# Modulation weights of pairs 1 to 7 in 2 MB chunks with buffers of their own, and two chunks at the RWKV block's entry

## The chip, the core and the metric

The kernel runs on one core of one Trainium2 chip. The metric is the device time of one execution in microseconds. The engines that matter: TensorE (PE in the profile: products; PEld: its weight loads), VectorE (DVE), ScalarE (ACT), GpSimd (POOL) and SyncE (SP), whose queue issues most loads.

## The reference, cut to what matters

One inference step of a two-layer trunk for 256 prompt tokens and 8 sequences of 8 sample tokens, together 320 columns (T), with 1024 features (8 tiles of 128). Everything is float32. Each layer is a feed-forward part, a token mixer (layer 0: RG-LRU, layer 1: RWKV-7) and a second feed-forward part. Every sub-layer takes a normed input with shift, scale and gate that come from a conditioning vector c:

```python
mod = (jax.nn.silu(c) @ P['ada_w'][layer] + P['ada_b'][layer]).reshape(B, N_MOD, D_MODEL)
sh1, sc1, g1, sh2, sc2, g2, sh3, sc3, g3 = [mod[:, m, None, :] for m in range(N_MOD)]
x = x + FFN_RES * (1.0 + g1) * swiglu(modulate(x, sh1, sc1), P['ffn_w_in'][layer, 0], P['ffn_w_out'][layer, 0])
h = modulate(x, sh2, sc2)
...   # y = the token mixer of h
x = x + (1.0 + g2) * y
x = x + FFN_RES * (1.0 + g3) * swiglu(modulate(x, sh3, sc3), P['ffn_w_in'][layer, 1], P['ffn_w_out'][layer, 1])
```

There are 9 conditioning rows (1 prompt, 8 samples) and 18 modulation vectors of 1024 for both layers. Their weights are 2 x 1024 x 9216 float32, 75 MB, the largest single weight beside the feed-forward ones.

## The kernel before, in words

The program is a list of items. An item has weight blocks and a function that issues its instructions. `Weights` loads the blocks, in the order of the items, through SyncE's queue into a ring of 5 raw buffers of 512 KB (`rawp`, L64). Blocks of dense products are then split into two exact parts, hi on ScalarE (L75) and lo on VectorE (L76), with two pairs of buffers; modulation blocks are used as they come and hold their raw buffer until their products are done. A load waits until the buffer five blocks back is free.

A dense product (`mm3`, L163 to L165) is three passes over 8 tiles of the contraction, 24 products of 128 x 128 weights with 320 (or 330) columns for a block.

The modulation vectors are made in 9 pairs (p = 0 to 8; p holds vectors 2p and 2p + 1), long before each is used. A pair has 8 steps, one for a tile of the contraction. A step (`Ada.step`) has two blocks, one for each vector of the pair, and four products (L179): the silu of c as weights of 32 columns, 512 columns of the block as the moving side, and each product writes its own 32 of the 128 rows of one PSUM bank. After the last step VectorE copies the sums (`ada_sb`, L184), and `finish` turns them with four products (L191) and adds the bias on VectorE (L197, L203).

Pair 0 is made first. The steps of the others are spread as items between those of the big parts (`interleave`): pairs 1 and 2 in the first half of layer 0's first feed-forward part, pair 3 in the RG-LRU block, pairs 4 and 5 in layer 0's second feed-forward part, pair 6 in layer 1's first one. Pairs 7 and 8 are thread "A" of the RWKV block. There, the string `MID` says which thread takes the next step: R, v, V are projections, p0 to p7 the preparation of the eight feature tiles, I, s, X, D, Z the inverse of triangular blocks (s on VectorE, X on TensorE), a0 to a7 the samples, C and G the chunks of the recurrence.

A scheduler then sets each engine's order from the items' order and its own estimate of when operands are there, so the instructions of neighbouring items can mix; after that every engine works its queue in order.

The entry of the RWKV block: the last out product of layer 1's first feed-forward part (`outm`), the residual, the squares on ScalarE (L244), two products with ones (L247, L248) for the norm's sums, then `start` with loads of constants on ScalarE's queue (L610) and the root and reciprocal (L265, L266), then `hd` and `part` for the first two tiles on VectorE, ScalarE and GpSimd, and `k_outer` (L833 to L837), the first products.

In `prep` (p0 to p7) the tile kk has one buffer: VectorE writes it (L769), ScalarE copies it into Dp (L780), and TensorE reads Dp (g, L803) and kk (dt, L822).

## Time and profile before

| | |
|---|---|
| time, median of 3 runs | 1502.36 us (1501.66 to 1503.32) |
| the profiled execution, first to last instruction | 1503.8 us (the page gives this span and no other time of its own) |
| TensorE busy | 1451.2 us, 97% |
| VectorE, ScalarE busy | 868.5 us (58%), 672.7 us (45%) |
| modulation products (L179) | 576 records, 101.1 us of TensorE |
| loads | 256.31 MB on SyncE's and ScalarE's hardware queue 1, 51.4% of the 16 DMA engines' time |

In rows of groups stands: line, engine, operation, what is written and read, shapes, count, then busy time and the mean of one in ns, then the idle time before them and who ended it. A row of the timeline is start, length, engine, line, names, count, and in brackets the idle time before it. A row of stretches is the stretch, its length, then for PE, PEld, DVE, ACT and POOL the busy time with the number of instructions in brackets, then the granted TensorE clock as a share of full speed, the share of the DMA engines and GB/s; where such a view is for one line, it holds only the engines which that line uses. A float32 product leaves two records in the trace, a product with the split parts one.

### The profile page before, as it was taken

How to read it: one execution, taken by the hardware profiler on the slowest of the kernel's cores; microseconds unless marked ns; L12 is line 12 of the kernel's file. 1: busy time of each engine (PE TensorE's matmuls, PEld its weight loads, DVE VectorE, ACT ScalarE, POOL GpSimd, SP SyncE). 2: the span in 40 equal slices, each digit the busy share in tenths (PEclk: the TensorE clock that was granted, in tenths of full speed). 3: DMA queues.
4: the chain of work that ended last, by engine and by line, in shares of the span. 5: the costliest groups of instructions: out<-in, count | busy, mean ns of one | idle time of the engine just before them, and what ended most of it. 6: DMA issues, size and time to landing. Idle time of an engine off the chain costs nothing.

```text
span 1503.8 us, 26002 instructions
## 1 busy us (share of the span) xinstructions
PE 1451.2 (97%) x10408; PEld 1306.0 (87%) x10408; DVE 868.5 (58%) x1667; ACT 672.7 (45%) x1215; POOL 65.1 (4%) x173
## 2 busy tenths in 40 slices
PE   5999999999999999999999997999998999999997
PEld 1888899988989889999999997597766779999996
DVE  6544445588874345566444447686763589544444
ACT  4433333487553333444333334475435446444432
POOL 0000000021000000000000003000022010000000
PEclk9999999999999999999999998999999999999998
DMA  8666744466467664545564545224765144444452
GB/s 338 234 244 239 247 138 152 151 231 224 153 233 248 238 242 140 154 152 201 205 223 140 151 140 173 102 90 159 219 207 177 51 147 141 142 153 154 139 148 72
DMA packets 93881, 266.58 MB, mean 177 GB/s; under 512 B 26368, under 2 KB 28800, under 8 KB 93248
## 3 DMA queue, kind: packets, MB, share of 16 engines
q1 hardware_dynamic: 84688, 256.31, 51.4%
q10 hardware_dynamic: 8976, 8.35, 1.7%
q8 instruction: 81, 1.33, 0.4%
q0 software_dynamic: 96, 0.26, 0.1%
q14 instruction: 40, 0.33, 0.1%
HBM read 257.86 MB, written 7.03 MB: 176 GB/s over the span
## 4 chain that ended last, share of the span: by engine, by line
PE 87%; DVE 6%; ACT 2%; DMA 2%; issue 1%; POOL 1%; ACTq 0%; DVEq 0%; SPq 0%; POOLq 0%
PE po L165 8%; PE po L163 8%; PE po L164 8%; PE pg L163 7%; PE pu L163 7%; PE pg L165 7%; PE pg L164 7%; PE pu L165 7%; PE pu L164 7%; PE ada_ps L179 5%; PE g L803 1%; DVE lo L76 1%; PE ps_l L687 1%; PE ps_p L163 1%; PE ps_p L165 1%
## 5 line engine op out<-in xcount | busy, mean ns | idle before, releaser
L75 ACT CAST hi<-raw 128x1024 fp32r<-128x1024 f32 (+1 forms) x334 | 341.8, 1023 | 613.2 <-issue 195.1
L76 DVE TENSOR_TENSOR lo<-raw,hi 128x1024 fp32r<-128x1024 f32 (+1 forms) x334 | 398.2, 1192 | 351.8 <-ACT hi L75 350.5
L163 PE MATMUL po<-hh,hi 128*128 128x320 f32 x704 | 217.2, 309 | 0.0
L165 PE MATMUL po<-hh,lo 128*128 128x320 f32 x704 | 217.2, 309 | 0.0
L164 PE MATMUL po<-hl,hi 128*128 128x320 f32 x704 | 217.2, 309 | 0.0
L163 PE MATMUL pu<-mh,hi 128*128 128x320 f32 x608 | 189.3, 311 | 0.7 <-ACT hi L75 0.7
L163 PE MATMUL pg<-mh,hi 128*128 128x320 f32 x608 | 189.8, 312 | 0.0
L165 PE MATMUL pg<-mh,lo 128*128 128x320 f32 x608 | 187.6, 309 | 0.0
L165 PE MATMUL pu<-mh,lo 128*128 128x320 f32 x608 | 187.6, 309 | 0.0
L164 PE MATMUL pg<-ml,hi 128*128 128x320 f32 x608 | 187.6, 308 | 0.0
L164 PE MATMUL pu<-ml,hi 128*128 128x320 f32 x608 | 187.6, 308 | 0.0
L163 PEld LDWEIGHTS po<-hh,hi 128*128 128x128 f32 x704 | 132.0, 187 | 0.0
L165 PEld LDWEIGHTS po<-hh,lo 128*128 128x128 f32 x704 | 132.0, 187 | 0.0
L164 PEld LDWEIGHTS po<-hl,hi 128*128 128x128 f32 x704 | 132.0, 187 | 0.0
L163 PEld LDWEIGHTS pg<-mh,hi 128*128 128x128 f32 x608 | 114.0, 187 | 16.8 <-issue 16.8
L163 PEld LDWEIGHTS pu<-mh,hi 128*128 128x128 f32 x608 | 114.0, 187 | 11.9 <-issue 8.4
L165 PEld LDWEIGHTS pg<-mh,lo 128*128 128x128 f32 x608 | 114.0, 187 | 0.8 <-DVE u L380 0.8
L164 PEld LDWEIGHTS pu<-ml,hi 128*128 128x128 f32 x608 | 114.0, 188 | 0.0
L164 PEld LDWEIGHTS pg<-ml,hi 128*128 128x128 f32 x608 | 114.0, 188 | 0.0
L165 PEld LDWEIGHTS pu<-mh,lo 128*128 128x128 f32 x608 | 114.0, 187 | 0.0
L179 PE MATMUL ada_ps<-raw,sct 128*32 128x512 f32 x576 | 101.1, 613 | 11.6 <-ACT sct L1277 7.2
L356 DVE TENSOR_TENSOR u<-pu,g 128x320 f32<-128x320 f32 x76 | 37.4, 492 | 109.7 <-PE pu L165 109.6
(358 smaller groups left out, 2375.6 us busy)
## 6 DMA issues: line engine op xcount, KB each, us to landing
raw<-in_ffn_in SPq DMA_DIRECT2D x176, 512.0 KB, 3.6
raw<-in_ada_w SPq DMA_DIRECT2D x144, 512.0 KB, 4.2
raw<-in_ffn_out SPq DMA_DIRECT2D x64, 512.0 KB, 3.6
raw<-in_ffn_out SPq DMA_DIRECT2D x32, 384.0 KB, 3.1
raw<-in_rkv SPq DMA_DIRECT2D x18, 512.0 KB, 4.2
raw<-in_lru_in SPq DMA_DIRECT2D x16, 512.0 KB, 4.2
raw<-in_lru_out SPq DMA_DIRECT2D x8, 512.0 KB, 3.3
raw<-in_wkv SPq DMA_DIRECT2D x8, 512.0 KB, 4.6
```

The source lines that it names most:

```text
L75: self.nc.scalar.copy(out=hi[:, :n], in_=raw[:, :n])
L76: self.nc.vector.tensor_tensor(out=lo[:, :n], in0=raw[:, :n], in1=hi.bitcast(F32)[:, :n], op=ALU.subtract)
L163: nc.tensor.matmul(ps[:, :n], a, xh[:, k0 + k, :n], start=st, stop=False)
L164: nc.tensor.matmul(ps[:, :n], a, xl[:, k0 + k, :n], start=False, stop=False)
L165: nc.tensor.matmul(ps[:, :n], b, xh[:, k0 + k, :n], start=False, stop=sp)
L179: nc.tensor.matmul(self.ps[r:r + 32, :], sct[:, k, :], wh[:, q * 512:q * 512 + 512], start=(k == 0), stop=(k == NT - 1))
L356: nc.vector.tensor_tensor(out=u, in0=pu[:, :T], in1=st[key, "g"], op=ALU.mult)
L687: nc.tensor.matmul(o[:, :T], lw[:, c0:c1], t, **kw)
L803: nc.tensor.matmul(g[:, c - c0, h], Dp[:, c, h].rearrange("p e t -> p (e t)"), AR[:, c].rearrange("p e t -> p (e t)"), start=True, stop=True)
```

## The change

Pairs 1 to 7 no longer go through the raw ring. Their weights load as chunks: 4 to a pair, numbered n = 0 to 27, each two steps and both vectors, 2 MB in one load on SyncE's queue, into two buffers taken in turn (tags MPa and MPb of a new pool `ext`). These two tags were buffers of the RWKV block's pool; their later users there (`xm` of r, MP, zh, zl) now take them from `ext`. The load of chunk n is an item of its own, put three items behind the products of chunk n - 2, but at most 12 items ahead of its own products. The 8 products of a chunk are issued with high priority and kept in program order.

Chunks 24 and 25 (the first half of pair 7) go into layer 1's first feed-forward part behind pair 6; chunk 26 is issued by the norm between the last out product and the two products with ones; chunk 27 by the RWKV block's `start`, after the norm. The copy of pair 7's sums then waits for the last tile of k's operands (`copy7`), and its `finish` stands between the adapters' products (lora). In `MID` the ten A entries of pair 7 are gone and nothing else. Pair 8 stays as it was, in single blocks. To make room, the RG-LRU block's yh and yl take the buffers of xch and xcl.

```diff
+    ext = ctx.enter_context(tc.tile_pool(name="ext", bufs=1))
...
-        def step(self, w, k):
+        def step(self, w, k, copy=True):
             for h, wh in zip(self.halves, w):
                 for q in range(2):
                     r = 64 * h + 32 * q
-                    nc.tensor.matmul(self.ps[r:r + 32, :], sct[:, k, :], wh[:, q * 512:q * 512 + 512],
-                                     start=(k == 0), stop=(k == NT - 1))
-            if k == NT - 1:
...
+                    mm = nc.tensor.matmul(self.ps[r:r + 32, :], sct[:, k, :], wh[:, q * 512:q * 512 + 512],
+                                          start=(k == 0), stop=(k == NT - 1))
+                    tc.keep_in_program_order(mm)
+            if k == NT - 1 and copy:
+                self.copy()
...
                 if self.sc is None and i == NT - 1:
+                    if self.hook:
+                        self.hook()
                     self.ps = bank(6, [128, 512], "st_ps")
...
+    def chunk_load(n):
+        p, c = 1 + n // 4, n % 4
+        t = st["chunk", n] = ext.tile([128, 2, 2, 1024], F32, tag=("MPa", "MPb")[n % 2], name="ada_w")
+        nc.sync.dma_start(out=t, in_=I["ada_w"][p, 2 * c:2 * c + 2].rearrange("k h r n -> r k h n"))
+
+    def chunk_step(n, copy=True):
+        p, c = 1 + n // 4, n % 4
+        if c == 0:
+            st["ada", p] = Ada(p, (0, 1), stat)
+        t = st.pop(("chunk", n))
+
+        with tc.high_priority():
+            for k in range(2):
+                st["ada", p].step([t[:, k, h] for h in range(2)], 2 * c + k, copy)
...
+    def with_loads(items):
+
+        at = {chunks[fn]: j for j, (_, fn, *_) in enumerate(items) if fn in chunks}
+        before = {}
+        for n in sorted(at):
+            lo = at[n - 2] + 3 if n > 1 else at[0] - 4 + 2 * n
+            before.setdefault(max(min(lo, at[n]), at[n] - 12), []).append(n)
...
-            for n, dt in (("xc", F32), ("xch", F32R), ("xcl", F32R), ("r", F32), ("a", F32), ("th", F32), ("gb", F32), ("yh", F32R), ("yl", F32R)):
-                L[n] = P.tile([128, NT, T], dt, name="L" + n)
+            for n, dt in (("xc", F32), ("xch", F32R), ("xcl", F32R), ("r", F32), ("a", F32), ("th", F32), ("gb", F32)):
+                L[n] = P.tile([128, NT, T], dt, tag=n, name="L" + n)
...
+            if i == 0:
+                for n, tag in (("yh", "xch"), ("yl", "xcl")):
+                    L[n] = L["p"].tile([128, NT, T], F32R, tag=tag, name="L" + n)
...
             st["norm"].finish()
+            chunk_step(27, copy=False)
...
+        def copy7(w):
+            with tc.issue_after(R["lo", NT - 1]):
+                st["ada", 7].copy()
+
+        it(copy7)
         for i in range(NT):
+            if i == 2:
+                it(lambda w: st["ada", 7].finish())
             it(lambda w, i=i: lora(w, i))
...
-        for p in (7, 8):
-            if p == 8:
-                step("A", lambda w: st.update(ada_bank=3))
-            for bl, fn in ada_items(p):
-                step("A", fn, bl)
+        step("A", lambda w: st.update(ada_bank=3))
+        for bl, fn in ada_items(8):
+            step("A", fn, bl)
...
-    items.extend(interleave(a, ada_items(1) + ada_items(2), 2, 40))
+    items.extend(interleave(a, ada_chunks(1) + ada_chunks(2), 2, 42))
...
-    items.extend(interleave(lru, ada_items(3), 1, 33))
+    items.extend(interleave(lru, ada_chunks(3), 1, 33))
...
-    items.extend(interleave(a, ada_items(4) + ada_items(5), 2, 40))
+    items.extend(interleave(a, ada_chunks(4) + ada_chunks(5), 2, 42))
...
-    a, b = ffn_items(1, 0, 11, lambda: Norm())
-    items.extend(interleave(a, ada_items(6), 2, 40))
+    a, b = ffn_items(1, 0, 11, lambda: Norm(hook=lambda: chunk_step(26)))
+    items.extend(interleave(a, ada_chunks(6) + [chunk_item(n) for n in (24, 25)], 2, 42))
...
+    items = with_loads(items)
```

How this moves instructions is shown at three places. In the rows stand line, operation, what is written and read, shape, a count, and whose semaphores it waits for. The line numbers of the changed kernel differ: L179 becomes L180, L163 to L165 become L164 to L166, L803 becomes L857, L822 L876, L247 and L248 L254 and L255.

TensorE in layer 0's first feed-forward part, at the first stop for pair 1 (pu and pg are dense products). Before, and then now:

```order
L165 MATMUL pu<-xh,lo 128x330
L179 MATMUL ada_ps<-raw,sct 32x512 [waits DMAHW7_49,PE_49]
L179 MATMUL ada_ps<-raw,sct 32x512
L179 MATMUL ada_ps<-raw,sct 32x512 [waits DMAHW0_49]
L179 MATMUL ada_ps<-raw,sct 32x512
L163 MATMUL pg<-xh,hi 128x330 [waits Activation_49]
```

```order
L165 MATMUL pu<-xl,hi 128x330
L166 MATMUL pu<-xh,lo 128x330
L180 MATMUL ada_ps<-ada_w,sct 32x512 [waits DMAHW4_49,PE_49]
L180 MATMUL ada_ps<-ada_w,sct 32x512 x7
L164 MATMUL pg<-xh,hi 128x330 [waits Activation_49]
```

A stop had one step, four products with a wait for each of two loads; now it has two steps, eight products behind one wait, and there are half as many stops.

TensorE at the RWKV block's entry (po: the last out product; st_ps: the norm's sums; ps_k: k). Before, and then now:

```order
L165 MATMUL po<-hh,lo 128x320
L247 MATMUL st_ps<-acc,ones 128x320
L248 MATMUL st_ps<-sq,ones 128x320 [waits Activation_49]
L833 MATMUL ps_k<-xmxh,hi 128x320 [waits PE_49,Activation_49]
L834 MATMUL ps_k<-xmxh,lo 128x320 [waits DVE_49]
```

```order
L166 MATMUL po<-hh,lo 128x320
L180 MATMUL ada_ps<-ada_w,sct 32x512 [waits DMAHW7_49]
L180 MATMUL ada_ps<-ada_w,sct 32x512 x7
L254 MATMUL st_ps<-acc,ones 128x320
L255 MATMUL st_ps<-sq,ones 128x320 [waits Activation_49]
L180 MATMUL ada_ps<-ada_w,sct 32x512 [waits DMAHW5_49]
...
L887 MATMUL ps_k<-xmxh,hi 128x320 [waits PE_49,Activation_49]
```

Chunk 26 stands ahead of the statistics and chunk 27 (whose other seven products are left out) behind them. On ScalarE's queue the load of c_mask moves ahead of the last squares, and that of c_reset, which was issued earlier in the program, now stands between c_shift and the root.

TensorE in the RWKV block's preparation, between the g products of one tile and of the next (zw, za, pb, pn, dt, g: products of `prep`; ps_p: a projection, here of v). Before, and then now:

```order
L822 MATMUL dt<-eye,kk 128x128 x4
L179 MATMUL ada_ps<-raw,sct 32x512 [waits DMAHW1_49]
L822 MATMUL dt<-eye,kk 128x128 [waits Activation_49]
...
L179 MATMUL ada_ps<-raw,sct 32x512 [waits DMAHW2_49]
...
L741 MATMUL zw<-zwa,raw 128x320 [waits DMAHW5_49,DVE_49]
L179 MATMUL ada_ps<-raw,sct 32x512 [waits DMAHW6_49]
L793 MATMUL pb<-pr,c_bones 128x320 [waits DVE_49]
...
L743 MATMUL za<-zwa,raw 128x320 [waits Activation_49]
```

```order
L876 MATMUL dt<-eye,kk 128x128 x4
L795 MATMUL zw<-zwa,raw 128x320 [waits DMAHW3_49,DVE_49]
L164 MATMUL ps_p<-xmxh,hi 128x320
L876 MATMUL dt<-eye,kk 128x128 [waits Activation_49]
L165 MATMUL ps_p<-xmxl,hi 128x320
L166 MATMUL ps_p<-xmxh,lo 128x320
...
L847 MATMUL pb<-pr,c_bones 128x320 [waits DVE_49]
...
L797 MATMUL za<-zwa,raw 128x320 [waits Activation_49]
```

Where products of pair 7 stood between those of `prep`, products of the v projection stand now, which came further behind before.

More of the change, by code (lines that the diff above doesn't have):

```diff
@@ L178, in step, with copy @@
                     r = 64 * h + 32 * q
-                    nc.tensor.matmul(self.ps[r:r + 32, :], sct[:, k, :], wh[:, q * 512:q * 512 + 512],
-                                     start=(k == 0), stop=(k == NT - 1))
-            if k == NT - 1:
-                self.sb = self.pool.tile([128, 512], F32, tag="ada_sb", name="ada_sb")
-                r0, r1 = 64 * self.halves[0], 64 * self.halves[-1] + 64
-                nc.vector.tensor_copy(self.sb[r0:r1], self.ps[r0:r1])
+                    mm = nc.tensor.matmul(self.ps[r:r + 32, :], sct[:, k, :], wh[:, q * 512:q * 512 + 512],
[3 more added lines that the diff above has]
+                self.copy()
+        def copy(self):
+            self.sb = self.pool.tile([128, 512], F32, tag="ada_sb", name="ada_sb")
+            r0, r1 = 64 * self.halves[0], 64 * self.halves[-1] + 64
+            nc.vector.tensor_copy(self.sb[r0:r1], self.ps[r0:r1])
         def finish(self):
@@ L287, in fn @@
                     st["ada", p] = Ada(p, halves, stat)
-                st["ada", p].step(w, k)
+                with tc.high_priority():
+                    st["ada", p].step(w, k)
             out.append(([(I["ada_w"][p, k, h], False, 1024) for h in halves], fn))
@@ L292, in ada_items, with chunk_item, ada_chunks @@
         out.append(([], lambda w: st["ada", p].finish()))
+        return out
+    chunks = {}
+    def chunk_load(n):
[7 more added lines that the diff above has]
+        t = st.pop(("chunk", n))
+        with tc.high_priority():
+            for k in range(2):
+                st["ada", p].step([t[:, k, h] for h in range(2)], 2 * c + k, copy)
+    def chunk_item(n, fn=None):
+        fn = fn or (lambda w: chunk_step(n))
+        chunks[fn] = n
+        return [], fn
+    def ada_chunks(p):
+        return [chunk_item(4 * (p - 1) + c) for c in range(4)] + [([], None), ([], lambda w: st["ada", p].finish())]
+    def with_loads(items):
[4 more added lines that the diff above has]
+            before.setdefault(max(min(lo, at[n]), at[n] - 12), []).append(n)
+        out = []
+        for j, it in enumerate(items):
+            out.extend(([], lambda w, n=n: chunk_load(n)) for n in before.get(j, ()))
+            out.append(it)
         return out
@@ L412, in ffn_items @@
                           lambda w, m=m, k0=k0, nk=nk: outm(w, m, k0, nk)))
+        if l == 1 and s == 0:
+            chunks[b[-1][1]] = 26
         return a, b
@@ L628, in start @@
             st["norm"].finish()
-        it(start)
+            chunk_step(27, copy=False)
+        out.append(chunk_item(27, start))
         def hd(w, i):
@@ L704, in part_r @@
             if i == 0:
-                R["xm", 0] = pair((big, "x"), (R["p"], "MPb"))
+                R["xm", 0] = pair((big, "x"), (ext, "MPb"))
             part(i, 0, R["xm", 0])
@@ L719, in prep_start @@
             R["bv"] = P.tile([128, NT, T], F32, tag="bv", name="bv")
-            R["MP"] = {0: P.tile([128, 32, 2, 64], F32, tag="MPa", name="MP")}
+            R["MP"] = {0: ext.tile([128, 32, 2, 64], F32, tag="MPa", name="MP")}
             R["Dt"] = {}
@@ L734, in prep @@
             if i == 4:
-                R["MP"][1] = R["p"].tile([128, 32, 2, 64], F32, tag="MPb", name="MP")
+                R["MP"][1] = ext.tile([128, 32, 2, 64], F32, tag="MPb", name="MP")
             MP, MS = R["MP"][i // 4][:, 8 * (i % 4):8 * (i % 4) + 8], R["MS"][:, 2 * i:2 * i + 2]
@@ L1196, in comb @@
                 nc.scalar.dma_start(out=O["wkv_p"], in_=R["Su"])
-                R["zh"] = R["p"].tile([128, NT, T], F32R, tag="MPa", name="zh")
-                R["zl"] = R["p"].tile([128, NT, T], F32R, tag="MPb", name="zl")
+                R["zh"] = ext.tile([128, NT, T], F32R, tag="MPa", name="zh")
+                R["zl"] = ext.tile([128, NT, T], F32R, tag="MPb", name="zl")
                 R["pgs"] = bank(3, [128, NT, 64], "pgs")
```

17 lines of the change are left out of this document (8 added, 9 removed).

## The prediction

> **What bounds the kernel now.** I read the busy table of the page first, then its costliest groups.
>
> ```profile
> span 1503.8 us, 26002 instructions
> PE 1451.2 (97%) x10408; PEld 1306.0 (87%) x10408; DVE 868.5 (58%) x1667; ACT 672.7 (45%) x1215; POOL 65.1 (4%) x173
> L179 PE MATMUL ada_ps<-raw,sct 128*32 128x512 f32 x576 | 101.1, 613 | 11.6 <-ACT sct L1277 7.2
> ```
>
> TensorE (PE) is occupied for 97% of the span, so nearly everything that leaves its queue shortens the run. The third line is what the change touches: the modulation products at L179, 576 records (a float32 product leaves two records: 288 products), 101.1 us. Next, the entry of the RWKV block in the timelines of TensorE and ScalarE (ACT; ACTq is its queue issuing a load):
>
> ```profile
> 910.96 0.70 PE L247 MATMUL st_ps<-acc,ones 128*128 128x320 f32 x2
> 912.46 0.81 PE L248 MATMUL st_ps<-sq,ones 128*128 128x320 f32 x2 [0.80 <-ACT sq L244]
> 920.26 0.63 PE L833 MATMUL ps_k<-xmxh,hi 128*128 128x320 f32 x1 [6.99 <-ACT xmxh L663]
> ...
> 911.94 0.47 ACT L244 ACTIVATE sq<-x 128x320 f32<-128x320 f32 x1
> 913.42 0.45 ACTq L610 DMA_DIRECT2D c_shift<-in_shift  x1
> 913.92 0.53 ACT L265 ACTIVATE rstd<-st_ps,eps 128x320 f32<-128x320 f32 x1 [1.51 <-PE st_ps L248]
> ```
>
> There is one hole of 6.99 us, between the norm's statistics and the first k product, the longest of the span behind the start. ScalarE's root (rstd) starts at 913.92 although the statistics ended at 913.27: ScalarE's queue was still issuing loads until 913.87.
>
> **What one stop for modulation costs.** The timeline of TensorE around a stop in the first feed-forward part, then a stop of one product, and one of two steps together:
>
> ```profile
> 177.42 0.30 PE L165 MATMUL pu<-mh,lo 128*128 128x320 f32 x1
> 177.65 1.07 PE L179 MATMUL ada_ps<-raw,sct 128*32 128x512 f32 x8
> 178.65 0.41 PE L163 MATMUL pg<-mh,hi 128*128 128x320 f32 x1
> 178.90 0.31 PE L164 MATMUL pg<-ml,hi 128*128 128x320 f32 x1
> 179.05 0.31 PE L165 MATMUL pg<-mh,lo 128*128 128x320 f32 x1
> ...
> 300.19 1.05 PE L179 MATMUL ada_ps<-raw,sct 128*32 128x512 f32 x2
> ...
> 1033.71 1.92 PE L179 MATMUL ada_ps<-raw,sct 128*32 128x512 f32 x16
> 1035.56 0.49 PE L822 MATMUL dt<-eye,kk 128*128 128x128 f32 x2
> ```
>
> Dense products follow each other every 0.15 us (178.90 to 179.05). From the last one before the stop (177.42) to the second after it (178.90) are 1.48 us, where two steps of 0.154 would be 0.31: **a stop costs 1.17 us**. A stop of one product (x2) is occupied as long as one of four (1.05 against 1.07): the four products of a step write four groups of 32 rows and run side by side. Two steps together take 1.85 us to the next product, where one takes 1.00 (177.65 to 178.65): the second costs 0.85, so **a chunk costs 2.02 us** against 2.34 for two stops. How many stops each stage has comes from the busy time of L179 alone:
>
> ```profile
> 36.00:190.00 154.00, 17.05 (x128) 2.52 (x128) 0.98 0.69 239
> ...
> 300.00:362.00 62.00, 10.43 (x64) 1.75 (x64) 1.00 0.66 233
> ...
> 410.00:560.00 150.00, 18.09 (x128) 2.65 (x128) 1.00 0.69 240
> ...
> 670.00:790.00 120.00, 9.56 (x64) 1.39 (x64) 1.00 0.59 205
> ...
> 950.00:1066.00 116.00, 12.26 (x64) 1.98 (x64) 1.00 0.39 130
> 1066.00:1135.00 69.00, 15.59 (x64) 2.27 (x64) 1.00 0.70 211
> ```
>
> The first number after the stretch's length is TensorE's busy time. Divided by 1.06 it gives 16 stops, then 8 and one of two steps (8.48 + 1.92 = 10.4), 17, 9, ten (8 of one step or less, 2 of two), and 14.
>
> **The sum, stage by stage.** *Layer 0's first feed-forward part* (pairs 1, 2): 16 stops at 1.17 = 18.7 become 8 chunks at 2.02 = 16.2: **-2.5**. *Layer 0's second part* (pairs 4, 5): 17 stops = 19.9 become 16.2: **-3.7**. *Layer 1's first part*: 9 stops = 10.5 become four chunks of pair 6 and two of pair 7 = 12.1: **+1.6**. These stages have TensorE full, so I take the terms at face value, within 0.5 us in all:
>
> ```profile
> 36.00:190.00 154.00, 153.80 (x1026) 137.03 (x1026) 74.31 (x117) 57.96 (x93) 0.00 (x0) 0.98 0.69 239
> ...
> 400.00:700.00 300.00, 300.00 (x2016) 278.81 (x2015) 171.10 (x309) 128.53 (x212) 2.60 (x6) 1.00 0.60 199
> ```
>
>
> *RG-LRU block* (pair 3): nine stops, 8 x 1.17 + 2.02 = 11.4, become four, 8.1: -3.3. After its double stop TensorE also waits, and then its clock drops:
>
> ```profile
> 359.96 0.42 PE L163 MATMUL pb<-xh,hi 128*128 128x330 f32 x1 [1.53 <-ACT hi L75]
> ...
> 359.30:362.60 3.30, 1.76 (x9) 1.25 (x10) 3.30 (x8) 2.81 (x6) 0.21 (x2) 1.00 0.99 382
> 362.70:366.00 3.30, 3.30 (x14) 3.30 (x13) 3.18 (x9) 0.92 (x2) 2.03 (x2) 0.50 1.01 361
> 366.10:369.40 3.30, 3.30 (x23) 3.30 (x23) 1.96 (x4) 1.67 (x4) 0.00 (x0) 1.00 0.54 164
> ...
> 300.00:400.00 100.00, 97.00 (x616) 85.85 (x615) 85.59 (x216) 75.07 (x152) 18.32 (x44) 0.98 0.59 207
> ```
>
> The 1.53 us come from a late split of a weight block, whose buffer the modulation blocks had held; these no longer share the buffers. In the half-clock stretch (0.50) 14 products ran instead of 23, so 9 x 0.15 = 1.3 us. If both go, the gain is 3.3 + 1.5 + 1.3 = 6.1. Against that, VectorE (the third busy time of a row) works 85.6 of 100 us there, so it may become the limit. Bounds 2 and 6.1; I take **-4.0**, the middle.
>
> *RWKV entry.* Chunk 26 (2.0 us) goes between the last out product and the statistics. It starts where the first statistics product stood (910.96), so that product follows near 913.0 and the second, which waited for ScalarE's squares until 912.46, near 913.3: the statistics end 0.8 later, at about 914.1. ScalarE's queue carries one load issue more (c_reset, 0.45 as c_shift) and would start the root at about 914.35 in any case. Chunk 27 then lies in the hole of 6.99 us, whose end VectorE and ScalarE set. Price: **+0.4** (0 to 1). If the hole gave no cover, chunk 27 would add 2.0.
>
> *RWKV body.* Pair 7 leaves: ten stops, 8 x 1.17 + 2 x 2.02 = 13.4. Pair 8 comes in 12 stops instead of 14: 1.8. If TensorE stayed full, the gain would be 15.2. But its work there hangs on chains of VectorE. The prep of a tile writes kk (L769) into a single buffer, which the dt products of the tile before must have read, and then the inverse runs on VectorE:
>
> ```profile
> 1003.46 0.49 DVE L769 SCALAR_TENSOR_TENSOR kk<-tk,AR 128x320 f32<-128x320 f32 x1 [2.57 <-PE dt L822]
> ...
> 1011.81 0.48 DVE L769 SCALAR_TENSOR_TENSOR kk<-tk,AR 128x320 f32<-128x320 f32 x1
> ...
> 1024.47 0.49 DVE L769 SCALAR_TENSOR_TENSOR kk<-tk,AR 128x320 f32<-128x320 f32 x1 [1.39 <-PE dt L822]
> ...
> 1036.09 0.49 DVE L769 SCALAR_TENSOR_TENSOR kk<-tk,AR 128x320 f32<-128x320 f32 x1 [1.79 <-PE dt L822]
> ...
> 1044.68 0.48 DVE L769 SCALAR_TENSOR_TENSOR kk<-tk,AR 128x320 f32<-128x320 f32 x1
> ...
> 1114.85 0.19 DVE L891 TENSOR_TENSOR X<-X,tm 128x31 f32<-128x31 f32 x1
> ...
> 1118.42 0.74 PE L950 MATMUL xt<-eye,X 64*32 64x64 f32 x10
> ```
>
> Rounds of kk without a stop take 8.35 and 8.59 us, those with stops 12.66 and 11.62 (the latter holds four, 5.5 us): the stops lie on the path, but a round will not fall far under 8.4. The changed order also pulls products of v (24 x 0.154 = 3.7 us each) into those rounds, where the stops were. That work is then missing behind, where TensorE reaches the first product of X 3.4 us after VectorE has finished X (1115.04 to 1118.42). So at least 3 us should be gained, and at most 15.2. I take **-8.5**, a little under the middle, because the copy of pair 7's sums and its six small additions now also fall into the adapters' products (about 1.6 us of VectorE).
>
> Sum: -2.5 - 3.7 + 1.6 - 4.0 + 0.4 - 8.5 = **-16.7**. The profiled span is 1503.8, 1.4 above the median of the runs shown, 1502.4. So 1487.1 for a profiled span and **1485.7 us for the median**; I write 1485.5. Bounds for the median: with -2, +1 and -3 in the unsure terms 1494; with -6.1, 0 and -15.2 1476.5.
>
> **Loads.** The 2 MB loads go into SyncE's queue between the weight blocks, and each waits there until the products of the chunk two before have read its buffer.
>
> ```profile
> raw<-in_ffn_in SPq DMA_DIRECT2D x176, 512.0 KB, 3.6
> ...
> SPq L64 <- DVE lo L76: 828.6, 306, 8.6
> ...
> 915.70:919.00 3.30, 0.00 (x0) 0.00 (x0) 3.11 (x9) 1.09 (x2) 0.96 (x3) 0.50 0.95 374
> ```
>
> A weight load leaves when a split (lo, L76) frees its buffer. With five buffers and two split pairs it is about four blocks, 4 x 3.7 = 14.8 us, ahead of its own split, and lands in 3.6, so 11.2 us may lie ahead of it. 2.1 MB at the 374 GB/s of the last row are 5.6 us. I cost the loads at nothing; the number of bytes is the same as before.
>
> **Rivals.** *A: VectorE takes over.* The RG-LRU and RWKV blocks keep their length and only the feed-forward parts and the entry move: -2.5 - 3.7 + 1.6 + 0.4 = -4.2, 1498. For it: 85.6 of 100 us busy in the RG-LRU, the 8.4 us rounds. Against: rounds with stops are longer by just about the stops' cost. Chance 0.11.
>
> *B: slower, through SyncE's queue.* If a 2 MB load moves no faster than four single ones (4 x 3.6 = 14.4 us), every weight load behind it comes 3.2 us late, 26 times in the dense stretches: 83 us, so about 1570. It decides from 187 GB/s downwards (2.1 MB in 11.2 us). Against: 374 GB/s above. Chance 0.03. The Trainium skill bears on it ("DMA: Bandwidth & Descriptors", Queues, rings and completion order): each DMA engine consumes the descriptors of one issuing engine's ring in order. So a weight block cannot overtake the chunk ahead of it; by this only the lead in time protects it.
>
> *C: the clock holds at the entry.* If chunk 27 kept TensorE's clock up, some 22 k products would run at 0.15 instead of 0.27 us, 2.6 less: 1483. The traces speak against it: 359.30:362.60 shows TensorE busy 1.76 of 3.3 us, and half clock behind it. After chunk 27 some 4.5 us stay empty, so some stretch of 3.3 us has under 1.7 busy. Chance 0.04. The Trainium skill ("TensorE: Matmul & The Clock Gate", What's actually happening) says that half rate comes after at least one idle window of about 3.4 us. Taken as a window with no work at all, it would let the clock hold in part of the cases. The row at 359.30 disagrees, with a drop behind a window half at work, and the measurement decides.
>
> **How the numbers follow.** Forecast 0.82 (a gain of 8 to 26 us), A 0.11, C 0.04, B 0.03. The range is 1477 to 1495, the forecast's bounds; A and B are outside, C inside. 0.2% (3 us) is about what a measurement can tell from no change. Faster holds the forecast, C and most of A: 0.94; same 0.03, for the part of A that also loses the feed-forward gain; slower 0.03, B.
>
> **What would show it.** Right: 24 stops of 16 records before the RWKV block, each 1.9 us busy; 16 records in the hole after the statistics, and the first k product 0 to 1 us later behind the last out product; feed-forward parts shorter by 2.5 and 3.7 us; no half clock inside the RG-LRU block. The RWKV term is wrong if rounds of kk stay at 11 us or the hole between X and xt opens on the other side; everything is wrong if hi or lo of a weight block is waited for behind a chunk's load.

## The result, and the profile after

The changed kernel takes 1492.36 us (median of 4 runs, 1491.90 to 1493.83), the kernel before 1502.55 us (4 runs, 1501.66 to 1503.32). The ratio is 0.9924, 95% interval 0.9912 to 0.9936: a gain of 10.2 us by the medians and of 11.4 by the ratio (9.6 to 13.2), where 17 were forecast. In every run here the time is 1.8 us more than the span (1492.33 for the profiled span of 1490.5).

The first lines of the page of the changed kernel, the load of the chunks from its list of DMA issues, and the modulation products of the chunks alone (TensorE's busy time in stretches that hold the parts for pairs 1 and 2, 3, 4 and 5, 6 and half of 7, and the RWKV block's entry):

```profile
span 1490.5 us, 25826 instructions
PE 1431.5 (96%) x10408; PEld 1305.2 (88%) x10408; DVE 868.1 (58%) x1667; ACT 671.2 (45%) x1215; POOL 66.5 (4%) x173
...
ada_w<-in_ada_w SPq DMA_DIRECT2D x28, 2048.0 KB, 8.3
```

```profile
36.00:190.00 154.00, 15.39 (x128) 3.34 (x128) 0.99 0.73 272
300.00:362.00 62.00, 7.69 (x64) 1.67 (x64) 1.00 0.72 263
410.00:560.00 150.00, 15.39 (x128) 3.34 (x128) 1.00 0.65 242
660.00:830.00 170.00, 11.54 (x96) 2.50 (x96) 1.00 0.58 208
900.00:912.00 12.00, 3.85 (x32) 0.83 (x32) 1.00 0.63 201
```

The stops are as the prediction's sum has them: 8, 4, 8, 6 and 2 of 16 records, 1.92 us each. (That makes 26 before the entry; the 24 in the prediction's last paragraph miscounts its own sum.) TensorE is busy 19.7 us less, but idle for 6.4 us more (1503.8 - 1451.2 = 52.6 before, 1490.5 - 1431.5 = 59.0 now). The new idle time shows in TensorE's waits, first of the kernel before, then of the changed one (total us, times, longest):

```profile
PE pu L163 <- ACT hi L75: 1.7, 2, 1.0
...
PE po L163 <- ACT zh L1230: 0.5, 1, 0.5
```

```profile
PE x L1073 <- DMA XD<-xd_d: 5.1, 1, 5.1
PE ps_k L887 <- ACT xmxh L717: 4.5, 1, 4.5
PE po L164 <- ACT zh L1289: 4.5, 1, 4.5
...
PE pu L164 <- ACT hi L74: 3.5, 5, 0.7
```

Two waits of 5.1 and 4.5 us are new. Both lie in the RWKV block, behind the inverse: one for XD (the inverse X, written to DRAM and read back in another layout), one for zh, the operand of the out products.

To see where time came from, I took the same marks in every trace: starts of the first product of the norms' statistics, of the first k product, of the last kk on VectorE, the last step of X, the last xt product, the last pa product of the samples. The lengths between them, in us:

| stage | before | before, second profile | after | after - mean of before | predicted |
|---|---|---|---|---|---|
| 1 start and layer 0's first feed-forward part | 295.2 | 293.1 | 291.0 | -3.1 | -2.5 |
| 2 RG-LRU block | 119.7 | 119.6 | 116.3 | -3.3 | -4.0 |
| 3 layer 0's second feed-forward part | 254.4 | 254.5 | 252.1 | -2.4 | -3.7 |
| 4 layer 1's first part and the entry | 250.9 | 250.9 | 254.8 | +3.9 | +2.0 |
| 5 RWKV: to the last kk | 143.3 | 143.2 | 138.1 | -5.1 | |
| 6 to the end of X | 51.3 | 52.0 | 44.6 | -7.0 | |
| 7 to the last xt | 17.1 | 17.0 | 11.3 | -5.7 | |
| 8 to the samples' last pa | 79.7 | 77.3 | 85.6 | +7.1 | |
| 9 to the next norm's sums | 47.0 | 46.5 | 51.3 | +4.6 | |
| 5 to 9 together | 338.4 | 336.0 | 331.0 | -6.2 | -8.5 |
| 10 the rest | 245.2 | 245.2 | 245.4 | +0.2 | 0 |

(The second profile of the kernel before is from the experiments; the first was of an execution some 3 us longer than usual, so the mean of the two is the better base.) The RWKV term looks nearly right, but it is a difference of two large numbers: the block gained 17.8 us up to the end of the inverse and gave back 11.7 behind it.

**The gain.** VectorE's kk in the changed kernel, and the turn from X to xt on VectorE and TensorE:

```profile
1005.13 0.48 DVE L823 SCALAR_TENSOR_TENSOR kk<-tk,AR 128x320 f32<-128x320 f32 x1
1017.58 0.49 DVE L823 SCALAR_TENSOR_TENSOR kk<-tk,AR 128x320 f32<-128x320 f32 x1 [0.35 <-PE dt L876]
1025.55 0.49 DVE L823 SCALAR_TENSOR_TENSOR kk<-tk,AR 128x320 f32<-128x320 f32 x1 [0.48 <-PE dt L876]
...
1096.86 0.19 DVE L950 TENSOR_TENSOR X<-X,tm 128x31 f32<-128x31 f32 x1
...
1096.62 0.85 PE L1009 MATMUL xt<-eye,X 64*32 64x64 f32 x12
```

The round that had held four stops of pair 7 fell from 11.62 us to 7.97 (1017.58 to 1025.55). The round ahead of it did not: 12.45 us (1005.13 to 1017.58) against 12.66, although no stop is left in it, so it was not a stop that made it long. TensorE starts xt as soon as X allows it, where it came 3.4 us late before. Stages 5 to 7 as one stretch, before and then now, with the last two stops of pair 8 now:

```profile
920.26:1131.91 211.65, 207.43 (x1416) 158.40 (x1416) 146.90 (x344) 109.69 (x220) 25.30 (x82) 0.99 0.48 154
```

```profile
914.16:1108.19 194.03, 189.41 (x1344) 154.66 (x1344) 145.80 (x343) 108.95 (x220) 25.66 (x82) 0.99 0.38 121
...
1108.33 1.05 PE L180 MATMUL ada_ps<-raw,sct 128*32 128x512 f32 x4
...
1110.21 1.05 PE L180 MATMUL ada_ps<-raw,sct 128*32 128x512 f32 x4
```

TensorE is busy for 98% of both stretches; its busy time fell by 18.0 us and the length by 17.6. Of the 72 records that are gone, 64 are pair 7's. The other 8 are pair 8's: its last two stops now stand behind the stretch, so some 2.3 us (two stops at 1.17) of the gain here are a loss of stage 8.

**The loss, first place.** TensorE, VectorE and ScalarE in three stretches of 5 us, and how long the four reads of XD took to land, in the changed kernel; behind them the same of the reads before:

```profile
1115.00:1120.00 5.00, 3.77 (x60) 2.81 (x59) 0.00 (x0) 3.19 (x13) 1.72 (x4) 1.00 0.73 210
1120.00:1125.00 5.00, 0.00 (x0) 0.00 (x0) 0.00 (x0) 1.81 (x8) 0.46 (x1) 0.94 1.14 233
1125.00:1130.00 5.00, 4.92 (x33) 3.46 (x34) 1.38 (x2) 2.05 (x7) 1.24 (x2) 0.50 0.08 11
...
DMA to landing us min/median/max: 7.0/7.5/7.7
```

```profile
DMA to landing us min/median/max: 2.2/2.8/4.9
```

TensorE stands still for 5 us, with the DMA engines more than fully booked (1.14), and then runs at half clock. The reads take 7.5 us (median) instead of 2.8. In the changed kernel ScalarE's queue issues the reload of x (1280 KB, L1080) at 1116.78, just ahead of the reads (from 1117.97); before, it left at 1143.24, behind them (1138.13).

**The loss, second place.** The end of the RWKV block in the changed kernel, stretches of 10 us and TensorE's first out product:

```profile
1200.00:1210.00 10.00, 5.00 (x30) 3.74 (x28) 9.91 (x21) 1.75 (x6) 2.02 (x1) 0.99 0.61 216
1210.00:1220.00 10.00, 9.36 (x45) 9.13 (x46) 3.36 (x9) 2.56 (x5) 0.00 (x0) 0.67 0.00 0
...
1210.64 0.90 PE L164 MATMUL po<-zh,hi 128*128 128x320 f32 x2 [4.50 <-ACT zh L1289]
```

VectorE is busy 9.91 of 10 us and TensorE 5.00; then the clock is down to 0.67 on the mean. TensorE's order is another one here, in a place that the change does not touch. Before (pm, pv, pr: the samples' last norm; pgs: gates of the samples):

```order
L1207 MATMUL pgs<-sg,raw 128x64 x3
L1168 MATMUL pm<-AR,c_bones 128x512
...
L1176 MATMUL pv<-gn,c_sel 32x128 x4
L1183 MATMUL pr<-gnr,c_selT 128x128 x4
```

And now:

```order
L1227 MATMUL pm<-AR,c_bones 128x512
...
L1235 MATMUL pv<-gn,c_sel 32x128 x4
...
L1266 MATMUL pgs<-sg,raw 128x64 x6
L1242 MATMUL pr<-gnr,c_selT 128x128 x4
```

Before, the gates of the samples were done ahead of the samples' last norm, and VectorE could join the samples early; now six of them stand between pv and pr, and the samples' part (zh at L1289) comes last of all on VectorE.

### The profile page after: what moved, and what is told of

Same layout as the page of the kernel before. It is cut to its first block, busy times and chain, and to the rows that moved or that the text cites. A ratio compares the mean times of both kernels' runs of the same rounds, so it can differ in the third digit from the quotient of the medians.

```text
span 1490.5 us, 25826 instructions
## 1 busy us (share of the span) xinstructions
PE 1431.5 (96%) x10408; PEld 1305.2 (88%) x10408; DVE 868.1 (58%) x1667; ACT 671.2 (45%) x1215; POOL 66.5 (4%) x173
## 4 chain that ended last, share of the span: by engine, by line
PE 89%; DVE 5%; DMA 2%; ACT 2%; issue 1%; POOL 1%; DVEq 0%; ACTq 0%; SPq 0%
PE po L164 8%; PE po L166 8%; PE po L165 8%; PE pu L164 7%; PE pg L164 7%; PE pg L166 7%; PE pg L165 7%; PE pu L165 7%; PE pu L166 7%; PE ada_ps L180 4%; PE g L857 1%; PE ps_p L166 1%; PE ps_p L164 1%; PE ps_p L165 1%; PE ps_l L741 1%; DVE lo L75 1%
## 5 line engine op out<-in xcount | busy, mean ns | idle before, releaser
L164 PE MATMUL po<-hh,hi 128*128 128x320 f32 x704 | 217.2, 309 | 0.0
L166 PE MATMUL po<-hh,lo 128*128 128x320 f32 x704 | 217.2, 309 | 0.0
L165 PE MATMUL po<-hl,hi 128*128 128x320 f32 x704 | 217.2, 309 | 0.0
L164 PE MATMUL pu<-mh,hi 128*128 128x320 f32 x608 | 189.6, 312 | 1.5 <-ACT hi L74 1.5
L164 PE MATMUL pg<-mh,hi 128*128 128x320 f32 x608 | 188.3, 310 | 0.0
L166 PE MATMUL pu<-mh,lo 128*128 128x320 f32 x608 | 187.6, 309 | 0.0
L165 PE MATMUL pg<-ml,hi 128*128 128x320 f32 x608 | 187.6, 309 | 0.0
L165 PE MATMUL pu<-ml,hi 128*128 128x320 f32 x608 | 187.6, 309 | 0.0
L166 PE MATMUL pg<-mh,lo 128*128 128x320 f32 x608 | 187.6, 309 | 0.0
L164 PEld LDWEIGHTS po<-hh,hi 128*128 128x128 f32 x704 | 132.0, 187 | 0.0
L165 PEld LDWEIGHTS po<-hl,hi 128*128 128x128 f32 x704 | 132.0, 187 | 0.0
L166 PEld LDWEIGHTS po<-hh,lo 128*128 128x128 f32 x704 | 132.0, 187 | 0.0
L164 PEld LDWEIGHTS pu<-mh,hi 128*128 128x128 f32 x608 | 114.0, 187 | 12.9 <-ACT g L398 10.9
L164 PEld LDWEIGHTS pg<-mh,hi 128*128 128x128 f32 x608 | 114.0, 188 | 5.0 <-ACT hh L391 3.4
L166 PEld LDWEIGHTS pu<-mh,lo 128*128 128x128 f32 x608 | 114.1, 188 | 0.0
L165 PEld LDWEIGHTS pu<-ml,hi 128*128 128x128 f32 x608 | 114.0, 188 | 0.0
L165 PEld LDWEIGHTS pg<-ml,hi 128*128 128x128 f32 x608 | 114.0, 188 | 0.0
L166 PEld LDWEIGHTS pg<-mh,lo 128*128 128x128 f32 x608 | 114.0, 188 | 0.0
L180 PE MATMUL ada_ps<-ada_w,sct 128*32 128x512 f32 x448 | 53.9, 598 | 0.0
```

The lines of the kernel that those rows point to most:

```text
L164: nc.tensor.matmul(ps[:, :n], a, xh[:, k0 + k, :n], start=st, stop=False)
L165: nc.tensor.matmul(ps[:, :n], a, xl[:, k0 + k, :n], start=False, stop=False)
L166: nc.tensor.matmul(ps[:, :n], b, xh[:, k0 + k, :n], start=False, stop=sp)
L180: mm = nc.tensor.matmul(self.ps[r:r + 32, :], sct[:, k, :], wh[:, q * 512:q * 512 + 512], start=(k == 0), stop=(k == NT - 1))
```

## The experiments

Each was timed against the kernel before on the same chip, whose median was 1502.55 to 1505.29 from call to call, so the ratios are what to compare. Stages in us from one profile each, as in the table above (1 to 3, 4, 5 to 7, 8, 9).

| run | ratio to before (95%) | 1-3 | 4 | 5-7 | 8 | 9 |
|---|---|---|---|---|---|---|
| before, two profiles | 1 | 669.3, 667.1 | 250.9 | 211.7, 212.2 | 79.7, 77.3 | 47.0, 46.5 |
| changed kernel | 0.9924 (0.9912 to 0.9936) | 659.4 | 254.8 | 194.0 | 85.6 | 51.3 |
| steps_apart | 0.9970 (0.9959 to 0.9982) | 665.5 | 256.2 | 194.2 | 85.2 | 50.6 |
| pair7_back | 0.9998 (0.9989 to 1.0007) | 659.0 | 250.5 | 217.6 | 78.6 | 50.6 |
| pair7_loose | 0.9950 (0.9937 to 0.9962) | 659.4 | 250.5 | 211.7 | 77.9 | 46.8 |
| pair8_loose | 0.9940 (0.9927 to 0.9953) | 659.1 | 254.8 | 194.5 | 87.6 | 50.4 |
| x_write_act | 0.9923 (0.9910 to 0.9935) | 657.5 | 254.8 | 194.0 | 85.4 | 51.4 |
| reload_late | 0.9862 (0.9849 to 0.9876) | 659.1 | 254.8 | 194.0 | 80.7 | 46.3 |
| before_reload_late | 0.9961 (0.9948 to 0.9973) | 668.0 | 250.9 | 212.1 | 75.7 | 46.8 |
| tail_first | 0.9898 (0.9883 to 0.9913) | 658.8 | 254.8 | 194.0 | 84.1 | 48.5 |
| first_chunk | 0.9910 (0.9896 to 0.9924) | 659.2 | 254.8 | 194.0 | 84.8 | 51.2 |
| late_and_first | 0.9853 (0.9837 to 0.9869) | 660.1 | 254.8 | 194.0 | 82.3 | 47.0 |
| all_three | 0.9844 (0.9831 to 0.9858) | 657.2 | 254.9 | 194.0 | 79.4 | 47.5 |

### The kernel before, once more

> The kernel before, unchanged, for a second profile of it. In the changed kernel's runs the time is 1.8 us more than the span (1492.33 for a span of 1490.5). If that holds for the kernel before as well, its usual span is 1502.5 - 1.8 = 1500.7, and the profile that the prediction was built on (1503.8) was of an execution some 3 us longer than usual: this one should show a span of 1500 to 1501.5, and the difference to the first should sit in a place or two (I expect stretches of half clock). The rival: the span is again near 1503.8, and time and span stand differently to each other in this kernel.

Time 1500.92 us, span 1499.1 (0.9 below the expected range): the offset of 1.8 holds, and the first profile (1503.8) was of a long execution, some 3.2 us above the median (the prediction set its span beside the median time and made it 1.4; its forecast takes the gain off the median and does not change by this). The 4.7 us between the two lie in stage 1 and its start (2.1) and in stage 8 (2.4), all other stages agree within 0.7. In stage 1 it is the clock at the start of the dense products; the same stretch in the first and in the second profile:

```profile
38.00:42.00 4.00, 4.00 (x17) 4.00 (x17) 2.55 (x7) 1.21 (x3) 0.00 (x0) 0.52 0.72 229
```

```profile
38.00:42.00 4.00, 4.00 (x24) 4.00 (x24) 2.59 (x8) 2.15 (x6) 0.00 (x0) 0.81 0.45 147
```

At 0.52 there were 17 products, at 0.81 there were 24. In stage 8 the clock differs too: 0.72 on the mean from 1148 to 1160 in the first profile, 1.00 from 1146 to 1158 in the second.

### Does the pairing of steps pay?

```diff
-            for k in range(2):
+            for k in steps:
```

`steps` is (0,) in one item and (1,) in the next, for chunks 0 to 25. In layer 0's two feed-forward parts the items are spread up to item 40, as in the kernel before, and not 42.

> The changed kernel with the two steps of each chunk 0 to 25 as two items of four products, at places near those of the kernel before; loads in 2 MB and buffers of their own as in the changed kernel. Theory (the gain of the feed-forward parts is the pairing of steps): 26 chunks x (2 x 1.17 - 2.04 = 0.30) = 7.8 us longer, less up to three or four waits of 0.84 for a split of a weight block that the first single stops of a part cover (0.84 x 3 = 2.5): 5 to 8 us longer than the changed kernel, 1497 to 1500. Rival (the gain comes from the raw ring that the modulation blocks no longer hold): 0 to 2 us longer, 1492 to 1494.

As expected: 1498.82 us, by the ratios 0.46% or 6.9 us more than the changed kernel. Stages 1 to 4 are 7.5 us longer (921.6 against 914.2), stages 5 to 9 the same within 1.0. A part of the 3.4 in stage 1 is the clock (0.60 at 38 to 42 us, where the changed kernel has 0.88); stages 2 to 4 alone are 4.1 us longer for 18 chunks, where 0.30 each would be 5.4. Loads and buffers are those of the changed kernel, so most of what pays in the first four stages is that the two steps of a chunk share a stop.

### Pair 7 back in the RWKV block, and whole or loose steps

pair7_back takes `MID` and pair 7's single steps from the kernel before and drops chunks 24 to 27. pair7_loose differs from it by this, for the single steps of pairs 0, 7 and 8:

```diff
-                with tc.high_priority():
-                    st["ada", p].step(w, k)
+                st["ada", p].step(w, k, whole=False)
...
-                    tc.keep_in_program_order(mm)
+                    if whole:
+                        tc.keep_in_program_order(mm)
```

> The changed kernel with pair 7 as before: single blocks in the RWKV block's order, nothing at the entry, chunks for pairs 1 to 6 alone. The two profiles give for the move of pair 7: first feed-forward part of layer 1 +4.1 (two chunks), entry +0.4, RWKV block and out products up to the next norm -7.4 us. If that is right the time is 1492.4 - 4.1 - 0.4 + 7.4 = 1495 (1494 to 1497). If the RWKV block were bound by VectorE's chains and pair 7 had cost nothing there, the time would be 1488 (1487 to 1490). With my predicted 8.5 to 15.2 for the block it would be 1496 to 1503.

> The kernel of pair7_back (chunks for pairs 1 to 6, pair 7 in single blocks in the RWKV block), but the single steps of pairs 0, 7 and 8 without high priority and without a fixed order of their products, as in the kernel before; the RWKV block's order is then that of the kernel before. In pair7_back the block from the first k product to the next norm took 346.8 us, in the two profiles of the kernel before 338.4 and 336.0, with the same list of threads. Theory (stops that are kept whole and go first hold up the chains of the preparation): the block comes back to 336 to 339 and the time to 1494 to 1496.5. Rival (the buffers that moved to the pool ext, or the loads, make it longer): the block stays at 344 or more and the time at 1501 to 1504.

> The changed kernel, with the single steps of pairs 0 and 8 without high priority and without a fixed order, as in the kernel before. If whole stops that go first cost about 9 us in the block with both pairs in it (pair7_back), pair 8's twelve should cost a part of it: 1 to 4 us shorter than the changed kernel, 1488.5 to 1491.5. Rival (all of it was pair 7's, among the chains of the preparation; pair 8's stops lie beside the inverse): within 1 us, 1491.5 to 1493.5.

pair7_back was a miss: 1503.55 us, as slow as the kernel before, 6.5 us above the range. The gain of stages 1 to 3 was there, but the RWKV block had become longer than it ever was (346.8 us). pair7_loose then took 1495.16, as its theory says, with 336.5 us for the block. So a part of the change that I had neither described nor priced, the single steps of the raw ring that are now kept whole and go first (pair 8 did not stay just as it was), costs about 10 us (346.8 - 336.5) when pair 7 is in the block: 5.9 in the preparation and the inverse, 3.7 in stage 9. There TensorE also waits a little more for blocks that are still loading; first pair7_back, then pair7_loose:

```profile
PE ada_ps L181 <- DMA raw<-in_ada_w: 4.8, 7, 1.6
```

```profile
PE ada_ps L181 <- DMA raw<-in_ada_w: 3.0, 6, 1.0
```

For pair 8 alone it costs nothing: pair8_loose (1493.58) does not differ from the changed kernel by more than the intervals. And pair7_loose shows how little the move of pair 7 brought on balance: from it to the changed kernel, stage 4 pays 4.3, stages 5 to 7 gain 17.7, stages 8 and 9 pay 7.7 and 4.5; by these stages 1.2 us of gain are left, by the ratios 0.26%, 3.9 us. Against pair8_loose, which treats the single steps as pair7_loose does, it is 0.10%, 1.5 us, inside the intervals. By stages, 8.8 of the change's 10.9 us lie in stages 1 to 3, in the chunks of pairs 1 to 5.

### The round trip of X

```diff
-                (nc.sync if b else nc.scalar).dma_start(out=xd[b], in_=X[64 * b:64 * b + 64])
+                nc.scalar.dma_start(out=xd[b], in_=X[64 * b:64 * b + 64])
```

> The changed kernel with both halves of the inverse X written out from ScalarE's queue (L1018) and not one of them from SyncE's, where its issue stands at 1111.7 behind loads that wait for pair 8's products, 14.7 us after X is done. Theory (the round trip of X through DRAM took over as the wait): in the changed kernel TensorE waits 5.1 us for XD (1120.0 to 1125.1) and then runs 3.4 us at half clock. With the write about 6 us earlier the reads leave at about 1111.7, the wait shrinks to 0 to 1.5 us and the half clock goes: 4 to 7 us shorter, 1485.5 to 1488.5. Rival (what follows is set by VectorE and the samples' chain anyway): the idle time moves to the end of the recurrence (1204 to 1211), and the time stays within 1 us, 1491.5 to 1493.5.

The rival's number (1492.25), but not for the rival's reason: the wait did not move to the end. The writes left at 1103.6 and 1104.1, and two of the four reads at 1109.8 and 1110.1 instead of 1118.0; but the other two left at 1119.0 and 1119.3 all the same, and by then the reload of x had left again (1117.4). TensorE waited 5.1 us for them, up to 1124.6. The list of SyncE's waits names what released the third, the landing of another read of the written X; why it had to wait for that is open:

```profile
SPq L1024 <- DMA MP<-xd_d: 8.3, 1, 8.3
```

So the edit did not take the wait away, and it tells nothing on what would follow. The next one goes at what the reads share the DMA engines with:

```diff
+            nc.gpsimd.tensor_copy(out=X[0][0:32, 0, 0:32], in_=R["MP"][1][0:32, 16, 0, 32:64])
             nc.scalar.dma_start(out=X[0], in_=R["xd"])
```

With it the reload's step (L) moves in `MID` behind the last step that uses XD: `X Z Z L Q` where `X Z L Z Q` stood. before_reload_late has the same two edits.

> The changed kernel, with the reload of x (1280 KB, L1080) made to wait for the products that use XD, by a small copy ahead of it. In the changed kernel the reload leaves at 1116.8, one microsecond ahead of the reads of XD, which then land after 7.0 to 7.7 us; in the kernel before it left behind them, and they landed after 2.2 to 4.9. Theory (the round trip of X is bound by what else the DMA engines carry): the reads take about 4 us, TensorE's wait of 5.1 us falls to 1 or 2, and the half clock behind it goes: 3 to 5 us shorter, 1487.5 to 1489.5. Rival (in x_write_act the wait stayed whatever the write did, and the end is set by the chain behind it): within 1 us, 1491.5 to 1493.5.

> The kernel before, with the same late reload of x as in reload_late (which took 10.3 us off the changed kernel). Theory (in the kernel before the reads of XD were hidden behind pair 8's and the samples' products, landed in 2.2 to 4.9 us, and the order at the end was the good one, so there is nothing to win; the 10 us were a part of the change's own gain that it gave back): within 1.5 us of the kernel before. Rival (the late reload is an improvement of its own, which has nothing to do with the change): 5 us or more below the kernel before.

reload_late took 1482.13 us, 9.3 us less than the changed kernel by the ratios, more than its theory had. In its profile the reads of XD land in 3.2 us, and TensorE works where it stood still (behind the rows of reload_late, the first product with XD in the changed kernel):

```profile
DMA to landing us min/median/max: 2.9/3.2/3.4
...
1115.00:1120.00 5.00, 4.22 (x32) 3.47 (x33) 0.00 (x0) 1.66 (x7) 0.30 (x2) 0.51 0.41 93
1120.00:1125.00 5.00, 4.10 (x56) 2.92 (x54) 0.98 (x2) 4.49 (x18) 1.88 (x3) 0.81 0.43 87
1125.07 0.24 PE L1073 MATMUL x<-XD 32*32 32x32 f32 x2
...
PE po L164 <- ACT zh L1290: 0.5, 1, 0.5
```

```profile
1125.08 0.28 PE L1073 MATMUL x<-XD 32*32 32x32 f32 x2 [5.11 <-DMA XD<-xd_d]
```

Stage 8 is 4.9 us shorter, as the theory wants, but not by its way alone. The reads, issued from 1118.2 to 1119.7, had landed by about 1123; the first product with XD still starts at 1125.07, as in the changed kernel, because products of the samples now stand ahead of it in TensorE's order and fill the time. Nor did the half clock go: it lies earlier (0.51 at 1115 to 1120). And the length of the wait is not the price of the stage: in steps_apart and first_chunk, which change nothing in this block, TensorE waits 3.1 and 2.8 us for XD, and stage 8 takes 85.2 and 84.8. Stage 9 is 5.0 shorter too, which the theory had not foretold: the end of the block stands again as in the kernel before, and the wait for zh is 0.5. So the edit changed the reads and the scheduler's order at two places, and I cannot divide its gain by this run alone.

The control before_reload_late does not fit its theory: 1499.20, 0.39% or 5.9 us (4.1 to 7.8) below the kernel before, as the rival said. Its stage 8 is 4.0 and 1.6 shorter than in the two profiles; the rest is not seen in its one profile, whose span (1498.6) is hardly below the second of the kernel before. So I cannot call the whole 9.3 us a loss of the change: by the ratios some 3.4 (9.3 - 5.9, each uncertain by about 2) belong to it, and the rest is to be had without it too.

### The order at the end of the block

```diff
-        step("E", comb_s)
-        step("F", comb_t)
+        step("E", first(comb_s))
+        step("F", first(comb_t))
```

`first` runs a step at high priority; the steps of the samples' norm (G4) get the same.

> The changed kernel, with the samples' last chain at the end of the RWKV block (the head norm of the samples' chunk and the two steps that join it with the gate) at high priority, so that on VectorE it stands ahead of the prompt tiles' z, zh, zl. The runs so far fall in two classes behind the last sample product: 46.3 to 47.0 us to the next norm in the kernel before, pair7_loose and reload_late, 50.6 to 51.3 in the changed kernel and the others, by how the gate's and the samples' products stand in TensorE's order; in the changed kernel TensorE waits there 4.5 us for zh of the samples (VectorE 9.9 of 10 us busy) and then runs 5 us at half clock. Theory (it is this order, and not the modulation work, that gives back 4 to 5 us): 2 to 5 us shorter than the changed kernel, 1487.5 to 1490.5, with the wait for XD unchanged at about 5 us. Rival (VectorE has the same work to do before the last out product in any order): within 1 us.

As the theory says: 1489.03, 0.26% or 3.9 us less than the changed kernel, while TensorE still waits 5.1 us for XD. Stage 9 is 2.8 shorter (48.5), short of the good order's 46.3 to 47.0. With this, stage 9 falls in two classes over all runs: 50.4 to 51.4 where the samples come last, 46.3 to 47.5 with the order of the kernel before, and tail_first between. TensorE's wait for zh is 4.5 us in every run of the first class and 0.3 to 0.5 in the second. That the order alone costs some 3 us in this stage is shown by tail_first; why the scheduler arrives at one or the other is not.

### The first stop of a part

The first chunk of layer 0's second feed-forward part goes between the second and the third weight block, where a single stop stood before.

```diff
-    items.extend(interleave(a, ada_chunks(4) + ada_chunks(5), 2, 42))
+    items.extend(interleave(a, ada_chunks(4) + ada_chunks(5), 0, 42))
```

> The changed kernel, with the first chunk of layer 0's second and layer 1's first feed-forward part one place earlier, between the second and the third weight block, where a single stop stood before. In the changed kernel TensorE waits there 0.84 us for the split of the third block (412.07 and 664.11) and once more at 681.76 (0.89). Theory (a stop at that place costs nothing, since the split needs that time in any case): both waits go and perhaps the third, 1.7 to 2.6 us shorter, 1489.8 to 1490.7. Rival (the wait appears at the next split): within 0.5 us, 1491.8 to 1492.9.

In the changed kernel TensorE waits at this place; with the chunk there, it does not. The timeline of TensorE, first of the changed kernel, then of first_chunk:

```profile
412.07 0.31 PE L165 MATMUL pg<-xl,hi 128*128 128x330 f32 x1
413.06 0.42 PE L164 MATMUL pu<-xh,hi 128*128 128x330 f32 x1 [0.68 <-ACT hi L74]
```

```profile
412.51 0.32 PE L166 MATMUL pu<-xh,lo 128*128 128x330 f32 x1
412.75 1.92 PE L180 MATMUL ada_ps<-ada_w,sct 128*32 128x512 f32 x16
414.61 0.42 PE L164 MATMUL pg<-xh,hi 128*128 128x330 f32 x1
```

Stage 3 fell by 0.95 us (252.1 to 251.1). In layer 1's part, where eight items are spread and not twelve, the first chunk stayed where it was, so did both waits, and stage 4 stayed at 254.8; there the edit did not do what the expectation says. By the ratios the kernel is 2.1 us faster, an interval that holds 0.95 as well.

### Together

> reload_late and first_chunk together. They lie in different stages (-10.3 and -2.3 against the changed kernel), so if both readings are right they add: 1492.4 - 12.6 = 1479.8 (1478.5 to 1481). If the scheduler's order at the end of the RWKV block falls back to the other class, 1484 to 1486.

> late_and_first, with the samples' last chain at high priority as in tail_first, and pair 3's first chunk in the RG-LRU block earlier, behind its second weight block, where the changed kernel waits 0.84 us for a split (295.71). The RG-LRU stage should fall from 116.4 to about 115.5; the way from the last sample product to the next norm from 46.3 to 43 to 45 if that chain still sets it, or stay. Together 1 to 4 us below late_and_first: 1476 to 1479; the rival (VectorE's whole work there sets it) 1479 to 1480.

late_and_first takes 1482.79 (0.9853), all_three 1481.28 (0.9844): 1.8 and 2.3 us above the ranges, on a chip where the kernel before took 1505.29; by the ratios they are 1.4 and 2.7 us below reload_late, which the intervals do not part from it. The chunk for pair 3 behind the second weight block shortens the RG-LRU block from 116.4 to 115.7. The samples' chain at high priority brings nothing once the order is good (47.5 against 47.0): there the rival held. Both are faster than the changed kernel by more than their intervals, all_three by 0.8%, 12 us.

## Why the prediction was right or wrong

- **A chunk costs 2.02 us, a stop 1.17: right.** 2.04 in the changed kernel, and taking the pairs apart again cost 7.5 us in stages 1 to 4, some of it clock, where 26 x 0.30 = 7.8 was worked out.
- **Layer 0's first part, -2.5: right** (-3.1 from the mean, -2.1 from the second profile; the clock at the start is in both).
- **Layer 0's second part, -3.7: too much, -2.4.** The step that failed is that every stop of 17 costs 1.17. The first one stood where TensorE would have waited for the split of the third weight block anyway; without it 0.84 us of waiting appear at 412.07 (0.99 less a step of 0.15). first_chunk gives 0.95 back.
- **Layer 1's first part and the entry, +1.6 and +0.4: +3.9.** The entry is right: from the last out product to the first k product 9.82 us (904.34 to 914.16) against 9.45, so 4 us of products cost 0.4. The 1.9 missing are nearly two more such waits, at 664.11 and 681.76 (0.84 and 0.89); that a stop there would take them away is argued, since first_chunk did not reach them.
- **RG-LRU, -4.0: -3.3.** The wait of 1.53 and the half clock are gone, as said, and no half clock is left in that block (300 to 400: 1.00); but four other waits of 0.84 to 1.44 for splits took their place (at 295.71, 307.53, 374.39 and 381.94).
- **RWKV body, -8.5: -6.2, by a cancellation.** The step that failed is that TensorE's work there hangs on chains of VectorE, for which the term went from 15.2 to 8.5. TensorE was busy for 98% of the part up to the inverse before and after, and that part gained what "if TensorE stayed full" says: 17.8 us, of which 2.3 are pair 8's two stops that now lie behind it, so 15.5 against 15.2. The rounds of kk were misread: the one of 12.66 us stayed at 12.45 without a stop in it. "That work is then missing behind" named the right danger at the wrong place. I looked for it between X and xt, where the hole closed. It was missing 23 us later: TensorE's own backlog had covered the reads of XD, and now ran out ahead of them. At the end of the block the samples came last in VectorE's order. I took the middle of the bounds and did not follow the chain behind the inverse to its end. That the term comes near is luck.
- **Pair 8 in 12 stops instead of 14, -1.8:** the 12 are there, and two stops at 1.17 would be 2.3. Kept whole, the single steps cost some 10 us where pair 7 is among them, nothing for pair 8 alone. The edit has no price of its own in the prediction, which is a gap that did not show in the sum.
- **Loads cost nothing: right.** The 2 MB loads land in 8.3 us (5.6 forecast), 253 GB/s, still above the 187 GB/s of rival B, and no split waits for one. The weight load issued behind a chunk landed behind it in all 28 cases, as the prediction had it. Rival B is out. But a load that the change does not touch, the reload of x, did come to lie on other transfers.
- **Rival A (VectorE takes over):** wrong for the preparation; at the end of the block (9.91 of 10 us) VectorE does set the time, for 4.5 us.
- **Rival C (the clock holds at the entry): out.** From 914.16 the k products start every 0.27 us as before (914.59 to 914.86), until 919.4.

```profile
907.71 1.92 PE L180 MATMUL ada_ps<-ada_w,sct 128*32 128x512 f32 x16
914.16 0.63 PE L887 MATMUL ps_k<-xmxh,hi 128*128 128x320 f32 x1 [4.53 <-ACT xmxh L717]
914.59 0.47 PE L888 MATMUL ps_k<-xmxh,lo 128*128 128x320 f32 x1
914.86 0.47 PE L887 MATMUL ps_k<-xmxh,hi 128*128 128x320 f32 x1
```

In all: the time lies in the stated range because the feed-forward terms, where stops are counted on a full TensorE, were nearly right, and because two errors in the RWKV term nearly cancel. Of the 6 us missing, 3.2 lie in stages 3 and 4, where three waits for splits that a removed stop had hidden make 2.6, and 2.3 in the RWKV term.

## What to carry to other kernels

A stop on the busiest engine costs its full time only where nothing else is late at that moment: before counting it, ask for each place what would end the wait without it. When a stage becomes shorter, follow the chain to the end of the block, DMA round trips and the last VectorE chain included, since slack that covered them goes too. And where a scheduler sets the order, compare its order in places that the edit does not touch; a changed order at the end of a block was worth 4 to 5 us, nearly half of what the edit gained.

## What the runs showed of the hardware

In the changed kernel 5.1 us of waiting for XD were followed by a stretch at half clock (0.50 at 1125 to 1130), 4.5 us of waiting for zh by ten at 0.67 on the mean. The Trainium skill ("TensorE: Matmul & The Clock Gate", What's actually happening) says that the window that is watched is about 3.4 us long and runs freely, not from the kernel's start. That fits the granted clocks of one stretch in two executions of the same kernel (0.52 and 0.81 at 38 to 42 us). Sixteen runs of it spread from 1500.5 to 1505.3 us; that this comes from the clock is not shown.

Four reads of 64 KB took 7.0 to 7.7 us to land with a load of 1280 KB issued 1.2 us ahead of them, 2.9 to 3.4 us without it.
